# Scheduling priorities for the delta rule's chains and units, and a router that multiplies in four column tiles

## The chip, the cores and the metric

One program runs on one core of a Trainium2 chip. The metric is the device time of one execution in microseconds (us). Three runs of the kernel before took 2969.64, 2970.99 and 2975.12 us; the median is 2970.99 us.

## The reference, cut to what matters

The model has two layers on 512 latent tokens and 256 context tokens, 1024 wide. Each layer is a mixer, a residual, and an expert-choice feed-forward (16 experts, each takes the 64 latent tokens, and in layer 0 also the 32 context tokens, that score highest for it).

The router scores tokens before the experts can start:

```python
aff = jax.nn.softmax(jnp.einsum('bnd,de->bne', h, w_router), axis=-1)   # 1024 -> 16 columns
gate, idx = lax.top_k(jnp.swapaxes(aff, 1, 2), cap)
```

The mixer of layer 1 has a window attention (8 heads, blocks of 128 tokens) and a delta rule (RWKV-7: 8 heads of 64, forward and backward over the tokens):

```python
sa = einsum('bhvk,bhk->bhv', S, -kk)
S  = S * dec + sa[..., None] * (kk * a) + v[..., None] * k      # token after token
y  = einsum('bhvk,bhk->bhv', S, r)
```

Both results, side by side, are multiplied by an output matrix and added to the residual.

## The kernel before, in words

The program is: mixer 0 (to about 460 us), its output projection with the routers of layer 0 (`out_proj`, L741 on), the experts of layer 0 (`moe(0)`), mixer 1 (`mixer1`, about 1440 to 2230 us) with the routers of layer 1, and the experts of layer 1 (`moe(1)`).

A scheduler puts the instructions in order when the program is built. Every instruction has a priority, by default its place in the order in which the Python code issues it (its trace). On each engine the scheduler takes, of the instructions whose inputs are ready by its own clock, the one that was traced first. The result is one fixed order for each engine and each DMA queue: on the chip an engine waits at the head of its queue, also where a later instruction would be ready. Only TensorE in `moe` is written out by hand.

Mixer 1 is traced as rounds of a loop over Python generators (`while` at L1563). In one round every generator takes one step:

- `chain(d, u, j)` for each of four units (direction d, head group u): the serial part of the delta rule, two halves of three steps each (`an`, `RH`, `pu`, `UV`, `pn`, `N1`; L1416 to L1454) and one step for the output `ysb` (L1456 to L1474). There are 24 chains, six for each (d, u), each after the one before it.
- `prep(sl, ...)`: a unit of 128 tokens is made ready for its chain. It loads keys and rates (`AR`, `BK`, `UV`), makes the Gram matrices (`gr`), and inverts a triangular matrix by five doublings (`pf`, `Qc`, `px`, `X`, `Zbd`), and ends with `Zf` (L1412). There are 24 preps in two slots, in three once the front is done. A prep needs a free set of buffers, which the end of an earlier chain gives back.
- `front()`: projections (`pj`, L926), their features for the delta rule (`features`, L948 on), then the projections for the window attention. The features of head pair p reach a prep through DRAM.
- `win_attend` (L1176 on): 32 heads times blocks, one each round, from the round after the front's end. Its buffers lie where the front's were, and the PSUM pools are cut anew there (`open_ps(4, 2)`, L1587).
- when the window attention is done, the output weights `wo` are loaded into its place (L1599, L739); `finish(lt)` (L1478) normalizes a tile of `ysb`; `projected(t, halves)` (L1543) multiplies half a tile (window half `winT`, delta half `rwT`) by `wo`.

When all chains and `finish` are done, the slots' memory becomes the ring for the experts' weights: `x` is loaded back (L1632) and the first weight blocks (`we`, 2 MB each; L1914) follow on the same queue, SP. The ring holds six blocks, two more lie in a second pool. The routers of layer 1 run beside the last projections.

`route_tile` (L1664) norms a tile, transposes it (`htp`), scales it into `ht`, and multiplies: eight matmuls `lg` with a 128-column piece of `ht` stationary and 16 router columns moving (L1688). A float32 matmul is two passes in the trace, so a tile has 16 passes. The router columns `wr` lie in a pool that lives through the whole program, and are loaded by POOL's queue in `route_open` (L1661).

Of the kernel before, what the change touches and what calls it, by code (L numbers as in the profile page):

```python
# [11 lines left out]
F32 = mybir.dt.float32  # L12
# [87 lines left out]
class Kern:  # L100
# [690 lines left out]
    def mixer1(self):  # L791
# [325 lines left out]
        def front():  # L1117
            lats = [g for t in range(2, 6) for g in (inputs(t),)]

            def ahead():  # L1120
                if lats and next(lats[0], self) is self:
                    lats.pop(0)
            for a in (aC, aL):
                n = a[0].shape[2]
                lat = n == NLAT
                low = [fo.tile([128, n], F32, name=nm) for nm in ("tl", "al", "sgl")]
                for i, half in enumerate((1.0, None, 0.5)[:3 if lat else 2]):
                    yield from filled(shifted(12 + i, a, low[i]))
                    if half is not None:
                        nc.scalar.activation(low[i], low[i], AF.Tanh, scale=half)  # L1130
                    if i == 2:
                        nc.gpsimd.tensor_scalar(low[i], low[i], 0.5, 0.5, OP.mult, OP.add)
                for p in range(4):
                    kp, rp, vp = [fo.tile([128, n], F32, name=nm, bufs=2) for nm in ("ko", "ro", "vo")]
                    for blk, dst in ((4 + p, kp),) + (((p, rp),) if lat else ()) + ((8 + p, vp),):
                        for _ in shifted(blk, a, dst):
                            fill(FILL)
                            ahead()
                            yield
                    yield from drain()  # L1140

                    def feed(c, p=p, lat=lat, src=(kp, rp, vp), low=low):
                        s = slice(c, c + 256)
                        t0 = 2 + c // 128 if lat else 0
                        yield from features(p, t0, *[t[:, s] for t in src], [t[:, s] for t in low])
                        fed.update(((t0, p), (t0 + 1, p)))
                    work.extend(feed(c) for c in range(0, n, 256))
                if not lat:
                    yield from filled(window(aC, None))
                    while lats:  # L1150
                        ahead()
                        fill(FILL)
                        yield
                    yield from drain()

            wc = [fo.tile([128, NLAT], F32, name="wc", tag=tag, bufs=2) for tag in ("ko", "ro", "vo")]
            for i in range(2):
                nc.gpsimd.dma_start(wc[i], io["k_wc"][i])
            yield from filled(window(aL, wc))
            yield from drain()  # L1160
# [351 lines left out]
            nc.vector.tensor_tensor(ro, F[:, 1], ro, OP.mult)  # L1512

        step_ = lambda g: next(g, g) is not g
        fr = front()
        while not all((1, p) in fed for p in range(4)):
            step_(fr)
# [46 lines left out]
        while min(nj.values()) < 6 or fins or min(nfin) < 2 or win:  # L1564
            for k in units:
                if chains[k] is None and nj[k] < 6 and k + (nj[k],) in done:
                    chains[k] = chain(*k, nj[k])
                if chains[k] is not None and not step_(chains[k]):
                    chains[k] = None
                    nj[k] += 1  # L1570
                    sets.append(done[k + (nj[k] - 1,)][-1])
            for sl in slots:
                if sl.gen is None and sets:
                    ok = [k for k in units if np_[k] < min(6, nj[k] + 2)
                          and all((tile_of[k[0]][np_[k]], 2 * k[1] + i) in fed for i in range(2))]
                    if ok:
                        k = min(ok, key=lambda k: np_[k])
                        sl.gen = prep(sl, sets.pop(0), *k, np_[k])
                        np_[k] += 1
                if sl.gen is not None and not step_(sl.gen):  # L1580
                    sl.gen = None
            if fr is not None and not all([step_(fr) for _ in range(FRONT)]):
                fr = None
                fst.close()
                self.open_ps(*PS)
                mp2 = st_s.enter_context(tc.tile_pool(name="mx1b", bufs=1))
                rwT = late["rwT"] = mp2.tile([128, 4, NLAT], F32, name="rwT")  # L1587
                winT = late["winT"] = mp2.tile([128, 4, NLAT], F32, name="winT")
                self.gate_rows(1, 1, mp2)
                tc.swap_default_side()  # L1590
                slots += [open_slot(SLOTS[0] + i, st_r) for i in range(SLOTS[1])]
                sets += [open_set(SETS[0] + i, st_r) for i in range(SETS[1])]
                tc.swap_default_side()
                ww = st_w.enter_context(tc.tile_pool(name="winw", bufs=2))
                kvq = win_open(ww)
                win = [win_attend(ww, *kvq)]
            if fr is None:
                if not win and wo is None:
                    st_w.close()  # L1599
                    wo = self.out_weights(1, io["od_w_out"][0])  # L1600
                    late["fin"] = st_f.enter_context(tc.tile_pool(name="m1f", bufs=2))
                for lt in range(4):
                    if wo is not None and yset[lt] == 4 and not nfin[lt] and len(fins) < 2:
                        nfin[lt] = 1
                        fins.append((lt, finish(lt)))
            for lt, g in list(fins):
                if not step_(g):
                    fins.remove((lt, g))
                    nfin[lt] = 2
            if wo is not None and min(nj.values()) < 6:  # L1610
                if not proj:
                    ready = [t for t in (3, 4, 2, 5) if nfin[t - 2] == 2 and lack[t]] + [
                        t for t in (3, 4, 2, 5) if 4 in lack[t]]
                    if ready:
                        t = ready[0]
                        proj.append(projected(t, lack[t] if nfin[t - 2] == 2 else [4]))
                if proj and not step_(proj[0]):
                    proj.pop(0)
            win = [g for g in win if step_(g)]
# [34 lines left out]
    def route_open(self, l):  # L1654

        nc, io, tc = self.nc, self.io, self.tc
        self.rt_st = ExitStack()
        self.rtw = self.rt_st.enter_context(tc.tile_pool(name=f"rtw{l}", bufs=2))
        self.rgm, self.rsh = self.gmod(l, 1)
        self.rwr = self.small.tile([128, 8, 16], F32, name="wr", tag="wr", bufs=1)  # L1660
        nc.gpsimd.dma_start(self.rwr, io["moe_router"][l].rearrange("(k p) n -> p k n", p=128))  # L1661
        self.lgt = self.small.tile([128, 6, 16], F32, name="lgt", tag="lgt", bufs=1)

    def route_tile(self, l, t):  # L1664

        nc = self.nc
        v = 1 if t < 2 else 0
        xn = self.rtw.tile([128, D], F32, name="xn", bufs=2 if l == 0 else 3)
        self.norm_tile(self.x[t], xn)
        nc.scalar.dma_start(self.xnd[0][t] if t < 2 else self.xnd[1][t - 2], xn)  # L1670
        yield
        ht = self.rtw.tile([128, 8, 128], F32, name="ht")
        for k0 in range(0, 8, 4):
            pt = self.bank("htp")
            for i in range(4):
                nc.tensor.transpose(pt[:, 128 * i:128 * i + 128], xn[:, 128 * (k0 + i):128 * (k0 + i) + 128], self.ident)
            for i in range(4):
                k, p = k0 + i, pt[:, 128 * i:128 * i + 128]
                if k % 2:
                    nc.scalar.activation(ht[:, k], p, AF.Identity, bias=self.rsh[:, k, v:v + 1],  # L1680
                                         scale=self.rgm[:, k, v:v + 1])
                else:
                    nc.vector.tensor_scalar(ht[:, k], p, self.rgm[:, k, v:v + 1], self.rsh[:, k, v:v + 1],
                                            OP.mult, OP.add)
        yield
        lg = self.bank("lg")
        for k in range(8):
            nc.tensor.matmul(lg[:, 0:16], ht[:, k], self.rwr[:, k], start=k == 0, stop=k == 7)  # L1688
        nc.vector.tensor_copy(self.lgt[:, t], lg[:, 0:16])

    def moe(self, l, out=None):
# [460 lines left out]
```

## Time and profile before

| | us |
|---|---|
| median of three runs | 2970.99 |
| the profiled execution | 2972.21 |
| its span, first to last instruction | 2970.4 |
| PE busy / DVE busy / ACT busy / POOL busy | 2660.2 / 1322.9 / 742.6 / 471.4 |
| the granted clock of PE, mean | 0.954 |
| DMA moved | 779.47 MB, mean 262 GB/s |

The page gives busy time by engine. PE's busy time holds the latency of matmuls that overlap, so 90% busy is not 90% used. The page's slices show three kinds of stretch: the experts of layer 0 with PE at 9 tenths throughout, mixer 1 with no engine full, and the experts of layer 1 with DMA at 9 tenths and some 427 GB/s.

### The profile page before, as it was taken

What the parts mean: (1) busy time and instruction counts of PE and PEld (TensorE: products, weight loads), DVE (VectorE), ACT (ScalarE), POOL (GpSimd) and SP (SyncE); (2) the same over time, 40 slices, a digit from 0 to 9 for tenths busy, and PEclk for the clock granted to TensorE, in tenths of its full rate; (3) what the DMA queues carried; (4) which work ended last, traced back from release to release, by engine and by line L of the source; (5) the groups of instructions that cost most, each with busy time, mean ns of one, the idle gap of its engine ahead of it and who ended that gap; (6) DMA issues with size and microseconds to landing.
All of it is one profiled execution on the core that took longest, in us unless ns stands there. A gap on an engine that the chain in (4) does not pass through costs nothing.

```text
span 2970.4 us, 47837 instructions
## 1 busy us (share of the span) xinstructions
PE 2660.2 (90%) x19606; PEld 1535.4 (52%) x19606; DVE 1322.9 (45%) x3546; ACT 742.6 (25%) x1718; POOL 471.4 (16%) x591
## 2 busy tenths in 40 slices
PE   7999999799999999999878878799987987888886
PEld 4787776544444444444466656587653332333322
DVE  4323665444234334322475777677654332223312
ACT  3212444211111111101354544366321111101111
POOL 2332003200000000000283553411210000000000
PEclk9999999799999999999987988899987999999999
DMA  9765001488988988988642233310349999999997
GB/s 329 244 246 175 27 12 57 172 333 353 371 356 355 371 345 367 365 355 355 216 126 73 86 108 120 111 32 28 118 184 377 426 427 427 427 426 427 426 427 314
DMA packets 176587, 779.47 MB, mean 262 GB/s; under 512 B 24327, under 2 KB 110768, under 8 KB 133488
## 3 DMA queue, kind: packets, MB, share of 16 engines
q1 hardware_dynamic: 169200, 752.31, 64.5%
q0 software_dynamic: 3872, 12.52, 1.2%
q10 hardware_dynamic: 3296, 11.58, 1.0%
q8 instruction: 155, 2.54, 0.4%
q14 instruction: 64, 0.52, 0.1%
HBM read 745.68 MB, written 30.67 MB: 261 GB/s over the span
## 4 chain that ended last, share of the span: by engine, by line
PE 64%; DMA 19%; DVE 9%; POOL 3%; ACT 3%; issue 2%; SPq 0%; POOLq 0%; ACTq 0%; DVEq 0%
PE gu L1924 13%; PE ydn L1992 9%; DMA wd<-in_moe_w_down_dram 8%; DMA we<-in_moe_w_gate_up_dram 8%; PE guc L1937 6%; PE ydc L1996 3%; PE pj L926 3%; PE pj L411 2%; PE pj L412 2%; PE pj L413 2%; PE op L774 2%; PE op L1556 2%; PE adap L231 2%; PE sc L593 1%; PE scp L1816 1%
## 5 line engine op out<-in xcount | busy, mean ns | idle before, releaser
L1924 PE MATMUL gu<-we,xs 128*64 128x512 f32 x3072 | 687.9, 597 | 83.5 <-DMA we<-in_moe_w_gate_up_dram 83.4
L1924 PEld LDWEIGHTS gu<-we,xs 128*64 128x64 f32 x3072 | 216.7, 137 | 520.5 <-issue 408.5
L1992 PE MATMUL ydn<-wd,uT 128*64 128x512 f32 x1536 | 351.8, 600 | 14.3 <-DMA wd<-in_moe_w_down_dram 13.7
L1930 DVE TENSOR_TENSOR sg<-gu,sg 64x512 f32<-64x512 f32 x96 | 66.5, 693 | 458.4 <-ACT sg L1929 457.8
L1929 ACT ACTIVATE sg<-gu 64x512 f32<-64x512 f32 x96 | 56.8, 592 | 846.3 <-PE gu L1924 846.3
L1776 POOL DMA_INDIRECT xg<-xnd,idx x22 | 20.9, 952 | 1246.6 <-DVE gate L1781 1186.0
L1992 PEld LDWEIGHTS ydn<-wd,uT 128*64 128x64 f32 x1536 | 107.9, 137 | 205.3 <-issue 187.0
L1937 PE MATMUL guc<-we,xs 128*32 128x256 f32 x3072 | 172.6, 380 | 0.0
L926 PE MATMUL pj<-aL,wblk 128*128 128x512 f32 x504 | 158.1, 448 | 0.0
L1937 PEld LDWEIGHTS guc<-we,xs 128*32 128x32 f32 x3072 | 96.4, 110 | 68.4 <-issue 7.5
L411 PE MATMUL pj<-ah,wblk 128*128 128x384 f32 (+1 forms) x320 | 109.5, 343 | 1.4 <-ACT ah L380 1.4
L926 PEld LDWEIGHTS pj<-aL,wblk 128*128 128x128 f32 x504 | 99.0, 210 | 18.4
L412 PE MATMUL pj<-al,wblk 128*128 128x384 f32 (+1 forms) x320 | 107.9, 338 | 0.0
L413 PE MATMUL pj<-ah,wblk 128*128 128x384 f32 (+1 forms) x320 | 107.4, 336 | 0.0
L1819 DVE TENSOR_TENSOR x<-scp,x 128x512 f32<-128x512 f32 x144 | 92.3, 684 | 30.3 <-PE scp L1817 29.4
L1996 PE MATMUL ydc<-wd,uTc 128*32 128x256 f32 x1536 | 90.6, 380 | 1.4 <-DMA wd<-in_moe_w_down_dram 1.4
L1906 DVE COPY uTc<-utc 128x128 f32<-128x128 f32 x48 | 14.0, 291 | 172.6 <-PE utc L1904 172.1
L2046 DVE TENSOR_TENSOR yp<-ydn,gbc 64x512 f32<-64x512 f32 x64 | 44.1, 689 | 103.8 <-PE ydn L1992 103.3
L1796 DVE TENSOR_SCALAR xs<-xst,gm,modT 128x128 f32<-128x128 f32 (+1 forms) x88 | 34.8, 397 | 118.9 <-PE xst L1788 115.7
L1900 ACT ACTIVATE uT<-utp 128x256 f32<-128x256 f32 x96 | 36.0, 375 | 159.4 <-PE utp L1899 158.6
L1382 DVE STREAM_TRANSPOSE Zbd<-X 64x256 f16<-64x256 f16 x144 | 62.7, 436 | 24.2 <-ACT X L1376 21.8
L1996 PEld LDWEIGHTS ydc<-wd,uTc 128*32 128x32 f32 x1536 | 47.6, 110 | 43.9 <-issue 15.2
(421 smaller groups left out, 4630.4 us busy)
## 6 DMA issues: line engine op xcount, KB each, us to landing
we<-in_moe_w_gate_up_dram SPq DMA_DIRECT2D x192, 2048.0 KB, 13.5
wd<-in_moe_w_down_dram SPq DMA_DIRECT2D x95, 2048.0 KB, 11.8
adaw<-in_ada_w_dram SPq DMA_DIRECT2D x48, 1024.0 KB, 6.5
wraw<-in_od_w_in_dram SPq DMA_DIRECT2D x33, 512.0 KB, 4.2
wraw<-in_ev_w_in_dram SPq DMA_DIRECT2D x19, 512.0 KB, 6.8
fb<-B SPq DMA_DIRECT2D x24, 256.0 KB, 2.5
BK<-fb SPq DMA_DIRECT2D x24, 256.0 KB, 3.0
xnd<-xn ACTq DMA_DIRECT2D x10, 512.0 KB, 4.7
```

The lines of the kernel that those rows point to most:

```text
L231: nc.tensor.matmul(pb[32 * j:32 * j + 32], self.spad[:, k, :], w[:, 512 * j:512 * j + 512], start=k == 0, stop=k == 7, tile_position=(0, 3 ...
L411: nc.tensor.matmul(pb[:m, :384], w[:, 0, k, 0:m], ah[k][:, t], start=k == 0, stop=False)
L412: nc.tensor.matmul(pb[:m, :384], w[:, 0, k, 0:m], al[k][:, t], start=False, stop=False)
L413: nc.tensor.matmul(pb[:m, :384], w[:, 1, k, 0:m], ah[k][:, t], start=False, stop=k == 7)
L926: nc.tensor.matmul(pb[:, :n], w[:, i, k], a[j][:, k], start=k + i + j == 0, stop=k == 7 and i == 1)
L1382: nc.vector.transpose(Zd[h], X[hd[h]])
L1819: nc.vector.tensor_tensor(xs, pb, xs, OP.add)
L1924: nc.tensor.matmul(gu[64 * j:64 * j + 64, :], g.xs[:, k, 64 * a:64 * a + 64], ws[j][k], start=k == 0, stop=k == 7, tile_position=(0, 64 * j))
L1930: nc.vector.tensor_tensor(sg, gu[64:128], sg, OP.mult)
L1937: nc.tensor.matmul(guc[32 * j:32 * j + 32, 0:256], q.xs[:, k, 32 * a4:32 * a4 + 32], ws[j // 2][k][:, 256 * (j % 2):256 * (j % 2) + 256], ...
L1992: nc.tensor.matmul(y[64 * h:64 * h + 64, :], uT[:, f], wt[i][:, 512 * h:512 * h + 512], start=f == 0, stop=f == 11, tile_position=(0, 64 * h))
L1996: nc.tensor.matmul(yc[32 * j:32 * j + 32, 0:256], uTc[:, f], wt[i][:, 256 * j:256 * j + 256], start=f == 0, stop=f == 11, tile_position=(0 ...
```

## The change

Two edits. In `mixer1` the steps of chains and preps are traced at a higher priority: their instructions count as if they had been traced 4000 (chains) or 3000 (units, the preps) places earlier. The Python flow, the instructions and their data stay the same.

In the router the operands change places: the router columns, padded with zeros to 32, are stationary in one of four column tiles, and `ht` moves through (128 columns); eight such matmuls leave four partial sums of the transposed logits in one PSUM bank. ACT copies the bank out (`ls`), and one matmul with a matrix of four stacked identities (`rsum`) adds the four parts and turns them. The router columns move from the long-lived pool to the router's own, which exists only while the routers run.

```diff
+        CHAIN, UNIT = 4000, 3000
+        def first(g, ahead):
+            with tc.high_priority(offset=ahead):
+                return step_(g)
...
-                if chains[k] is not None and not step_(chains[k]):
+                if chains[k] is not None and not first(chains[k], CHAIN):
...
-                if sl.gen is not None and not step_(sl.gen):
+                if sl.gen is not None and not first(sl.gen, UNIT):
...
-        self.rwr = self.small.tile([128, 8, 16], F32, name="wr", tag="wr", bufs=1)
-        nc.gpsimd.dma_start(self.rwr, io["moe_router"][l].rearrange("(k p) n -> p k n", p=128))
+        self.rwr = self.rtw.tile([128, 8, 32], F32, name="wr", bufs=1)
+        nc.gpsimd.memset(self.rwr[:, :, 16:32], 0.0)
+        nc.gpsimd.dma_start(self.rwr[:, :, 0:16], io["moe_router"][l].rearrange("(k p) n -> p k n", p=128))
+        self.rsum = self.rtw.tile([128, 16], F32, name="rsum", bufs=1)
+        nc.vector.tensor_tensor(self.rsum, self.ident[:, 0:16], self.ident[:, 32:48], OP.add)
+        for j in (2, 3):
+            nc.vector.tensor_tensor(self.rsum, self.rsum, self.ident[:, 32 * j:32 * j + 16], OP.add)
...
+        lp = self.bank("lgp")
+        for i in range(2):
+            for j in range(4):
+                nc.tensor.matmul(lp[32 * j:32 * j + 32, 0:128], self.rwr[:, 4 * i + j], ht[:, 4 * i + j], start=i == 0,
+                                 stop=i == 1, tile_position=(0, 32 * j))
+        ls = self.rtw.tile([128, 128], F32, name="ls")
+        nc.scalar.activation(ls, lp[:, 0:128], AF.Copy)
+        yield
         lg = self.bank("lg")
-        for k in range(8):
-            nc.tensor.matmul(lg[:, 0:16], ht[:, k], self.rwr[:, k], start=k == 0, stop=k == 7)
+        nc.tensor.matmul(lg[:, 0:16], ls, self.rsum, start=True, stop=True)
         nc.vector.tensor_copy(self.lgt[:, t], lg[:, 0:16])
```

## Rows read from the trace of the kernel before

**Rows 1.** Busy time by stage: us from:to, length, PE, PEld, DVE, ACT, POOL, PEclk, DMA, GB/s.

```profile
1540.00:1912.00 372.00, 304.78 (x2462) 233.06 (x2462) 251.94 (x558) 158.63 (x386) 177.69 (x246) 0.86 0.32 94
1912.00:2097.00 185.00, 165.31 (x1849) 141.46 (x1848) 129.80 (x396) 111.40 (x334) 37.79 (x60) 0.95 0.17 51
2097.00:2203.00 106.00, 95.06 (x988) 60.40 (x988) 66.32 (x152) 29.62 (x82) 21.35 (x27) 0.89 0.33 115
2203.00:2257.50 54.50, 35.77 (x148) 24.01 (x148) 22.85 (x70) 11.58 (x26) 8.05 (x11) 0.69 0.92 358
2257.50:2970.40 712.90, 601.28 (x2813) 225.18 (x2812) 206.67 (x595) 82.83 (x165) 10.33 (x13) 0.99 0.98 414
```

**Rows 2.** SP's queue from 2060 to 2420 us: start, us, line, what was issued.

```profile
2096.69 1.02 SPq L739 DMA_DIRECT2D wo<-in_od_w_out_dram  x2
...
2201.73 1.74 SPq L1632 DMA_DIRECT2D x<-xd  x4
2203.52 1.96 SPq L1914 DMA_DIRECT2D we<-in_moe_w_gate_up_dram  x3
2230.57 0.33 SPq L255 DMA_DIRECT2D brow<-in_ada_b_dram  x1
...
2231.89 1.73 SPq L1914 DMA_DIRECT2D we<-in_moe_w_gate_up_dram  x3
```

**Rows 3.** Chain of waits, 2090 to 2262 us, in order of time: start, us, what.

```profile
2110.87 5.78 PE op L1556 x8
...
2170.80 3.52 PE op L1556 x8
...
2199.68 1.99 PE yt L1503 x32
...
2205.78 9.57 PE op L1556 x16
2215.36 1.75 PE htp L1676 x16
2217.10 3.44 PE op L1556 x8
2220.54 3.25 PE lg L1688 x30
...
2229.27 0.91 DVE op L1560
```

**Rows 4.** Stage table for line L1412 (the end of a prep): DVE busy, count.

```profile
1540.00:1912.00 372.00, 5.08 (x12) 0.86 0.32 94
1912.00:2097.00 185.00, 2.94 (x7) 0.95 0.17 51
2097.00:2203.00 106.00, 2.11 (x5) 0.89 0.33 115
```

**Rows 5.** Groups by line, 1440 to 2262 us: a doubling's steps; busy, mean ns.

```profile
L1382 DVE STREAM_TRANSPOSE Zbd<-X 64x256 f16<-64x256 f16 x144 | 62.7, 436 | 24.2 <-ACT X L1376 21.8
L1366 DVE TENSOR_TENSOR Qc<-pf,lev 128x256 f16<-128x256 f32 x120 | 47.8, 415 | 10.4 <-PE pf L1285 9.7
L1376 ACT ACTIVATE X<-px 128x256 f16<-128x256 f32 x96 | 34.8, 383 | 61.6 <-PE px L1285 50.1 <-DVE GA L1331 4.8 <-issue 2.9
```

**Rows 6.** Groups by line, 1912 to 2097 us: the window attention's matmuls; busy, mean ns.

```profile
L1200 PE MATMUL sw<-kd,qw 128*128 128x256 f32 (+1 forms) x160 | 45.3, 398 | 7.7 <-DMA qw<-wqd 6.2 <-ACT Pw L1211 1.5
L1236 PE MATMUL po<-Vw,PTw 128*128 128x64 f32 x288 | 37.8, 278 | 0.5 <-DVE GR L1331 0.4
L1224 PE MATMUL ptw<-ks,Pw 128*128 128x128 f32 x144 | 22.4, 278 | 1.4 <-ACT KBt L1350 1.2
```

**Rows 7.** PE in order of time, 1712 to 1718 us: idle before it, and until what.

```profile
1712.82 0.71 PE L926 MATMUL pj<-aL,wblk 128*128 128x512 f32 x2
1716.53 0.69 PE L1440 MATMUL pu<-RH,Zf 64*64 64x64 f32 x8 [3.00 <-DVE RH L1435]
```

**Rows 8.** Chain of waits, 480 to 570 us: the output projection and routers of layer 0.

```profile
500.51 5.46 PE op L774 x24
505.97 1.69 PE lg L1688 x16
...
546.69 1.69 PE lg L1688 x16
548.38 5.57 PE op L774 x24
...
567.26 0.09 POOL wr L1661
...
568.19 0.21 POOL we L1834
```

**Rows 9.** The page's groups: matmuls in four column tiles, their weight loads; idle before them last.

```profile
L1937 PE MATMUL guc<-we,xs 128*32 128x256 f32 x3072 | 172.6, 380 | 0.0
...
L1937 PEld LDWEIGHTS guc<-we,xs 128*32 128x32 f32 x3072 | 96.4, 110 | 68.4 <-issue 7.5
```

**Rows 10.** Tiles winT, lg and wr: an ACT copy of 128x128 out of PSUM; durations min/median/max in ns; DMA landing.

```profile
L1246 ACT ACTIVATE winT<-orw x16: 268/269/283, 1944.1 to 2097.5; 128x128 f32<-128x128 f32 x16
...
L1688 PE MATMUL lg<-wr,ht x160: 177/263/396, 505.8 to 2240.6; 128*128 128x16 f32 x160
...
DMA to landing us min/median/max: 7.4/7.8/8.2
```

## The prediction

> **What bounds the kernel now.** I read the stage table first [rows 1]. From 2257.5 us to the end DMA is 98% busy at 414 GB/s: the experts of layer 1 are bound by their weights, at a fixed distance of 712.9 us from their first matmul. So nothing is won there, and everything ahead of it that comes earlier moves the end with it. From 1540 to 2203 us no engine is full: PE's clock is granted at 0.86 to 0.95, DVE is busy for 68%, 70% and 63% of the three stages. That stretch is bound by waits.
>
> Next, what lets the experts start. In SP's queue [rows 2] the first three weight blocks leave at 2203.52, right behind the loads of x, which wait for the last `finish` (`yt` at 2199.68 in the chain, [rows 3]); the other three leave at 2231.89, behind `brow`, which waits for the eviction of the last `op` matmul at 2229.27 [rows 3]. The blocks in flight cover the 28 us from there to the first expert matmul. The mark to move is therefore the end of the last `op`, call it T: 2229.3.
>
> Then, what holds T. The window attention ends at 2097 and `wo` is issued at 2096.69 [rows 2]; its first matmul runs at 2110.87, 14.2 us later [rows 3]. From there to T pass 118.4 us. `op` itself is 4 tiles x 2 halves of the columns x 8 k x 2 passes = 128 passes at 3.52/8 = 0.44 us [rows 3], 56.3 us. The other 62 us are the delta rule: 12 of the 24 preps have ended when the front ends, 7 more end in the window stage, and 5 end after 2097 [rows 4], with their chains, `finish`, and the last two halves of `op` behind them.
>
> Why are the preps late? Two slots gave 12 preps in 372 us, three slots 7 in 185: 62 and 79 us for one. A doubling's own steps are two transposes, one `Qc`, one `X`: 2 x 0.436 + 0.415 + 0.383 = 1.7 us [rows 5], and two groups of small matmuls; five doublings with head and tail are some 25 us (an estimate from these rows). More than half of a prep's time it waits for its turn, behind work that was traced earlier. This is what a priority acts on.
>
> **The change part by part.**
>
> *Priorities, front stage (to 1912).* The `open_ps` at the front's end cuts the PSUM pools anew. A prep traced behind it needs a bank of the new pools, so it can't pass the front's end, whatever its priority. Stepping through the loop, 14 of the 24 preps are traced before it. So the stage's work stays the same, two preps more get done in it at the most, and the front, which ends the stage, has later turns while preps run and freer engines once they are out. I take 0. Bounds: 10 us early (some in-order waits of PE go), 69 us late (the third rival).
>
> *Window stage.* 10 preps are left for it or what follows, and all of them now come ahead of the window attention. An offset of 3000 places reaches across the whole stage: PE, DVE, ACT and POOL together run some 2640 instructions and passes in it [rows 1]. The preps' cost here: PE is busy 165.3 us, the window's matmuls are 45.3 + 37.8 + 22.4 = 105.5 us of it [rows 6], which leaves 59.8 us for 7 preps and chains, 8.5 us each. Three more preps than before are 26 us on PE; PE is idle for 19.7 us of the stage [rows 1], and some of the 26 us fits there. I take half, 12 us: the window attention ends at 2109. Bounds: 5 us earlier than now, 26 us later. At three slots and 35 to 40 us a prep, 10 preps take some 130 us, so the chains end near 2060, well ahead of it.
>
> *After the window attention.* `wo` still comes 14.2 us later, and this time no prep covers the wait: PE idles and starts cold. The first 16 passes took 9.57 us after an idle stretch against 2 x 3.52 [rows 3], so 2.5 us are added. Then `op` runs through: 56.3 + 2.5, three tiles of transposes at 1.75/2 [rows 3], 2.6, three routers in the new form, 2.1 (below), and 3.5 for what isn't dense: 67 us in place of 118.4. What is late next is `wo`: since the slots come free before the window's end, weight blocks may be issued ahead of it on the same queue. One is 2 MB at 414 GB/s, 5.1 us [rows 1]; I take one block, 5 us; bounds none and four (20 us).
>
> T becomes 2096.7 + 12 + 14.2 + 5 + 67 = 2194.9, against 2229.3: -34.4 us.
>
> *Routers, layer 0.* Here PE is the path: `lg` stands four times in the chain, 1.69 us each, between `op` groups [rows 8]. The new form has again 16 passes, with 32 columns stationary and 128 moving. The nearest row is `guc`: 32 stationary, 256 moving, 172.6 us/3072 = 56 ns a pass, its weight loads 96.4/3072 = 31 ns [rows 9]. Half the columns give 28 ns if columns set the pace, 31 if the weight load does, 56 if neither; I take 31, the weight load's: 0.50 us, plus two passes of the last matmul at 1.69/16 = 0.11. That makes 0.71, and saves 0.98 x 4 = 3.9 us. Bounds: 56 ns gives 0.6 x 4 = 2.4 us; if PE also waits for the copy (0.27 us, [rows 10]) with nothing in front, 1 us is left. The copy itself lies on ACT beside `op`. The last tile's `lg` runs after its `ht`, where the chain copy-matmul replaces most of it: -0.3. The load of the next layer's `wr` no longer stands on POOL ahead of the copy that lets the second weight block go (567.26 to 568.19, [rows 8]): up to -0.9, of which I take 0.3. Together -4.5 us; the experts of layer 0 pass it on.
>
> By the Trainium skill, TensorEngine Tiling (Array Packing), Key Properties, a change of the tiling mode drains TensorE, which speaks against two changes more in each tile. The rows don't show it: `guc`, in four tiles and between matmuls in two, has 0.0 us idle before 3072 passes [rows 9], though a drain could hide in busy time. If each cost `lg`'s median duration, 0.263 us [rows 10], seven tiles on the path would lose 7 x 2 x 0.263 = 3.7 us and the time would be 2936.
>
> *Routers, layer 1.* Two tiles' `lg`, 3.25 us and a little, stand on PE ahead of the last `op` [rows 3]; that is already in the 67 us. The last tile behind T: -0.4. Against it stands the new load of `wr`: it landed in 7.4 to 8.2 us [rows 10], and can be issued only when the router's pool opens, when the last `finish` has left its memory. Now that would be about 2206, due before `lg` at 2220 [rows 3]; with `finish` early it is nearer to free. I take 0; bounds 0 and 5 us, as `op` queues behind a waiting `lp`.
>
> **Sum.** -34.4 - 4.5 - 0.4 = -39.3 us on the profiled 2972.2 (span 2970.4, 1.8 around it), 1.2 above the median of the runs: 2932 against 2971.
>
> **The rivals.**
>
> 1. *The window attention takes the preps' place as the last to end.* If it pays for all five preps that now end after 2097, at 8.5 us, it ends 42 us late in place of 12; with two blocks more ahead of `wo` (10 us), the time is 2932 + 30 + 10 = 2972, no change. For it: PE is busy 89% of the window stage [rows 1]. Against: that busy time holds latency, and DVE is at 70%. Chance 0.10.
> 2. *The order hardly changes.* The scheduler takes only what is ready, and preps that lag were traced early and so are first already; then the routers' 4.9 us and their 2.3 us on PE ahead of the last `op` are all: 2964. For it: no prep passes the front's end. Against: 62 to 79 us a prep. Chance 0.08.
> 3. *The front pays (slower).* Chain steps put ahead at times that the scheduler expected, not those of the chip, hold PE with the front's projections queued behind: at 1716.53 `pu` held PE for 3.00 us, waiting for `RH` behind feature work on DVE [rows 7]. Up to 23 chain halves run in the front stage; if each waited so long, the front would end 69 us late: 3001. It decides above 39 us, 13 such waits. Against: the priority holds on DVE too, and moves `RH` ahead of that feature work. Chance 0.10.
>
> **How the numbers follow.** The forecast, 2932, has 0.72; its own range is 2900 to 2960: window -5 and `wo` not delayed give -22, the front's 10 early would reach 2900; window +26, or `wo` behind four blocks, give 2946 and 2947, both about 2960. The range for 8 in 10 reaches to the second rival and stops short of most of the first: 2896 to 2966. Within 0.2% (6 us, about what a measurement can tell) lie the first rival and half of the second: 0.14. Slower is the third, 0.10; faster the rest, 0.76.
>
> **What would show it.** Right: the last prep's `Zf` near 2050 and not behind the window attention; `wo` issued between 2090 and 2125; a stretch of idle PE until it lands; then `op` dense at 0.44 us a pass; first expert matmul near 2218; four tiled router blocks of about 0.5 us in layer 0. Wrong: a front that ends after 1925, preps that still end behind `wo`, weight blocks ahead of `wo` on SP, or PE idle ahead of chain steps.

## The result, and the profile after

The changed kernel takes 2997.7 us (median of four runs, 2991.4 to 3000.4) against 2970.3 us before on the same chip: ratio 1.0090, 95% interval 1.0065 to 1.0115. Slower by 27 us, where 39 us faster was forecast. The profiled execution, the shortest of the four, took 2991.4 us with a span of 2989.6 us, 19.2 us more than that of before; its stages can show 19 of the 27 us.

The stages were cut anew, at events that both traces have: the last store of `wqd` (the front's end), the first row maximum of the window attention, the last `winT`, the first and the last `op`. Before (length, then busy us of PE, PEld, DVE, ACT, POOL, the granted clock, DMA share, GB/s):

```profile
1540.00:1911.50 371.50, 304.28 (x2456) 232.68 (x2458) 251.82 (x558) 158.13 (x386) 177.19 (x246) 0.86 0.32 94
1911.50:1926.10 14.60, 7.17 (x30) 5.35 (x30) 5.13 (x15) 2.60 (x7) 9.46 (x11) 0.62 0.78 242
1926.10:2097.80 171.70, 158.97 (x1832) 136.79 (x1831) 125.52 (x385) 110.06 (x330) 28.83 (x49) 0.98 0.12 35
2097.80:2110.80 13.00, 11.53 (x145) 10.04 (x144) 5.51 (x15) 7.00 (x20) 1.52 (x3) 0.64 1.00 377
2110.80:2230.00 119.20, 107.42 (x926) 63.87 (x924) 70.02 (x157) 28.22 (x75) 22.77 (x28) 0.90 0.39 144
```

After, the same stages, and the experts:

```profile
1540.00:1916.60 376.60, 299.48 (x2468) 225.58 (x2468) 254.28 (x559) 158.42 (x390) 174.67 (x244) 0.88 0.30 93
1916.60:1936.60 20.00, 7.30 (x16) 5.04 (x16) 4.98 (x11) 0.00 (x0) 9.56 (x11) 0.60 0.75 236
1936.60:2119.70 183.10, 163.82 (x1820) 142.39 (x1820) 125.33 (x384) 110.32 (x329) 28.99 (x49) 0.96 0.09 27
2119.70:2134.30 14.60, 11.95 (x148) 10.68 (x144) 6.13 (x16) 6.39 (x19) 2.46 (x4) 0.64 0.67 234
2134.30:2249.00 114.70, 106.11 (x937) 61.49 (x934) 70.03 (x156) 28.89 (x77) 22.61 (x30) 0.94 0.42 158
2276.20:2989.60 713.40, 603.02 (x2813) 225.35 (x2812) 206.73 (x595) 82.79 (x165) 10.33 (x13) 0.98 0.98 414
```

The counts are the first thing to read. The window stage has 1832 passes on PE before and 1820 after, 385 and 384 instructions on DVE: no work moved from the later stages into it. The same work takes longer: 5 us more in the front, 5.4 at its end, 11.4 in the window attention, 1.6 for `wo`, and 4.5 less in `op`. The experts keep their distance (713.4 us). The ends of the preps agree: still 12, 7 and 5 in the three stages, as in [rows 4] (DVE busy, count, clock, DMA share, GB/s):

```profile
1540.00:1916.60 376.60, 5.00 (x12) 0.88 0.30 93
1916.60:2119.70 203.10, 2.97 (x7) 0.93 0.15 47
2119.70:2249.00 129.30, 2.12 (x5) 0.91 0.45 167
```

The loss at the front's end is one of queue order. SP's queue before (start, us, line, what was issued):

```profile
1903.24 0.90 SPq L261 DMA_DIRECT2D gbc<-esd  x2
1906.95 2.54 SPq L1310 DMA_DIRECT2D AR<-fa  x4
```

and after:

```profile
1914.02 2.53 SPq L1310 DMA_DIRECT2D AR<-fa  x4
...
1917.23 0.94 SPq L261 DMA_DIRECT2D gbc<-esd  x2
```

POOL's queue before (start, us, line, what was done):

```profile
1911.37 2.35 POOL L262 TENSOR_TENSOR gbc<-gbc,brow 128x1024 f32<-128x1024 f32 x1
1915.68 3.08 POOL L1168 MEMSET kd<- 64x768 f32 x4
1918.71 0.64 POOL L1176 DMA_DIRECT2D band<-in_k_m_dram  x1
```

and after:

```profile
1923.18 2.34 POOL L262 TENSOR_TENSOR gbc<-gbc,brow 128x1024 f32<-128x1024 f32 x1 [1.25 <-DMA gbc<-esd]
1925.58 0.73 POOL L1168 MEMSET kd<- 64x768 f32 x1
1926.37 1.49 POOL L1341 TENSOR_TENSOR Ttbd<-GA,m 64x256 f32<-64x256 f32 x2
1927.94 1.40 POOL L1357 TENSOR_TENSOR Zbd<-Thbd,lev 64x256 f16<-64x256 f16 x2
1929.39 0.73 POOL L1168 MEMSET kd<- 64x768 f32 x1
1930.07 0.64 POOL L1176 DMA_DIRECT2D band<-in_k_m_dram  x1
```

On SP a prep's loads now stand ahead of `gbc`; POOL waits for `gbc` to land; then a prep's `Ttbd` and `Zbd`, moved ahead by the priority, stand between the two halves of the zeroing of `kd`; `band`, which the first score tile needs, leaves at 1930.1 in place of 1918.7. Counted from the front's end that is 13.4 us in place of 7.3: the multiplication of `gbc` with its wait is 3.6 us of the difference, `Ttbd` and `Zbd` are 2.9. Further on, SP's queue after shows `wo` cut in two, its second half 10.5 us late behind a prep's load (both halves left at 2096.69 in [rows 2]):

```profile
2119.49 0.39 SPq L739 DMA_DIRECT2D wo<-in_od_w_out_dram  x1
2126.08 2.56 SPq L1310 DMA_DIRECT2D AR<-fa  x4
2128.72 1.22 SPq L1317 DMA_DIRECT2D UV<-fv  x2
2130.00 0.59 SPq L739 DMA_DIRECT2D wo<-in_od_w_out_dram  x1
...
2227.25 1.83 SPq L1936 DMA_DIRECT2D we<-in_moe_w_gate_up_dram  x3
```

In the window stage the scores wait. PE's waits there (us in total, times, longest), before:

```profile
PE pf L1285 <- DVE X L1358: 2.5, 4, 1.1
PE sw L1200 <- ACT Pw L1211: 1.5, 3, 0.6
```

and after:

```profile
PE sw L1200 <- ACT Pw L1211: 12.5, 6, 5.3
PE pf L1285 <- DVE X L1358: 4.8, 4, 1.6
```

`sw` stands at the head of PE's queue and waits for the score tile that ACT's exponential (`Pw`) has not yet read; everything behind it on PE waits too, the preps' matmuls included. This wait is 10.8 to 13.6 us in the profiles of the four kernels that have both priorities in this stage and the window's own steps traced as before (after, e2, e3, e10 below), and 1.4 to 2.3 us in before, e1, e5, e6 and e9. Other waits went, so of the 11.4 us by which the stage is longer, PE is idle for 6.6 and busy for 4.9, at a granted clock of 0.96 in place of 0.98.

The routers of layer 0 stand in the chain as tiled matmuls ([rows 8] is before):

```profile
520.74 0.77 PE lgp L1703 x16
521.50 5.66 PE op L774 x24
527.16 0.13 PE lg L1710 x2
528.21 5.49 PE op L774 x24
533.70 0.77 PE lgp L1703 x16
...
584.23 1.05 PE gu L1946
```

A tile's period on PE, from one router to the next, is 12.96 us in place of 13.57. The first expert matmul comes at 584.2 in place of 587.8.

### The profile page after: what moved, and what is told of

Same layout as the page of the kernel before. It is cut to its first block, busy times and chain, and to the rows that moved or that the text cites. A ratio compares the mean times of both kernels' runs of the same rounds, so it can differ in the third digit from the quotient of the medians.

```text
span 2989.6 us, 47897 instructions
## 1 busy us (share of the span) xinstructions
PE 2659.0 (89%) x19626; PEld 1520.1 (51%) x19626; DVE 1330.1 (44%) x3552; ACT 743.1 (25%) x1728; POOL 470.2 (16%) x593
## 4 chain that ended last, share of the span: by engine, by line
PE 65%; DMA 18%; DVE 9%; POOL 3%; ACT 2%; issue 2%; SPq 0%; POOLq 0%; ACTq 0%; DVEq 0%
PE gu L1946 14%; PE ydn L2014 9%; DMA we<-in_moe_w_gate_up_dram 8%; DMA wd<-in_moe_w_down_dram 7%; PE guc L1959 6%; PE ydc L2018 3%; PE pj L926 2%; PE pj L411 2%; PE op L774 2%; PE pj L412 2%; PE pj L413 2%; PE op L1562 2%; PE adap L231 1%; PE sc L593 1%; PE scp L1838 1%
## 5 line engine op out<-in xcount | busy, mean ns | idle before, releaser
L1285 PE MATMUL pf<-X,Thbd 128*128 128x64 f16 x480 | 38.5, 201 | 35.0 <-DVE X L1358 32.8
## 6 DMA issues: line engine op xcount, KB each, us to landing
we<-in_moe_w_gate_up_dram SPq DMA_DIRECT2D x192, 2048.0 KB, 13.4
wd<-in_moe_w_down_dram SPq DMA_DIRECT2D x95, 2048.0 KB, 11.4
```

## The experiments

All ratios are to the kernel before on the same chip, with 95% intervals. The stage lengths are from each run's trace: *front*, from the first projection of mixer 1 to the last `wqd` store; *edge*, from there to the window's first row maximum; *window*, to the last `winT`; *tail*, to the end of the last `op` (T).

| kernel | median, us | ratio | front | edge | window | tail |
|---|---|---|---|---|---|---|
| before | 2970.3 | 1 | 449.1 | 14.6 | 171.7 | 131.4 |
| after | 2997.7 | 1.0090 (1.0065 to 1.0115) | 454.0 | 20.0 | 183.1 | 128.5 |
| e1 router alone | 2964.6 | 0.9975 (0.9963 to 0.9987) | 443.1 | 14.1 | 173.8 | 127.6 |
| e2 priorities alone | 3002.5 | 1.0106 (1.0089 to 1.0123) | 457.8 | 20.2 | 184.5 | 132.1 |
| e3 after, window opened first | 2991.0 | 1.0068 (1.0051 to 1.0085) | 459.5 | 14.2 | 183.5 | 128.5 |
| e4 after, banks split | 3090.1 | 1.0398 (1.0379 to 1.0418) | 455.4 | 31.2 | 300.5 | 89.1 |
| e5 router, chains' priority | 2984.2 | 1.0048 (1.0032 to 1.0065) | 456.6 | 14.0 | 175.9 | 137.5 |
| e6 router, units' priority | 2984.7 | 1.0058 (1.0040 to 1.0075) | 450.4 | 20.2 | 175.7 | 131.4 |
| e7 after, window moved too | 3031.4 | 1.0203 (1.0188 to 1.0218) | 451.5 | 16.1 | 226.6 | 130.7 |
| e8 router, banks split | 2976.4 | 1.0015 (1.0004 to 1.0025) | 442.5 | 19.5 | 171.2 | 143.6 |
| e9 priorities in the front only | 2978.8 | 1.0025 (1.0016 to 1.0035) | 455.8 | 15.0 | 176.2 | 127.9 |
| e10 priorities after the front only | 2987.0 | 1.0049 (1.0035 to 1.0064) | 445.4 | 21.7 | 187.4 | 130.5 |
| e11 router, window opened first | 2965.6 | 0.9983 (0.9970 to 0.9995) | 446.5 | 15.6 | 171.8 | 127.7 |
| e12 as e5, 100 places | 2984.7 | 1.0041 (1.0029 to 1.0054) | 453.7 | 15.1 | 173.7 | 138.2 |

**The two edits apart.** e1 is the kernel before with the router's hunks alone, e2 with the priorities alone.

> The kernel before with the router edit alone. If the loss lies in the priorities (my theory), the router edit keeps the gain that the profile after shows in layer 0 (first expert matmul 584.2 in place of 587.8 us, 3.5 us) and 1 to 2 us behind the last `op`: about 5 us faster than before, 2965. If the router edit is the loser (a rival: three more DVE instructions ahead of the norm, the load of `wr` behind the opening of the pool), this kernel is slower than before, 2975 or more.

> The kernel before with the priorities alone. If the loss lies in the priorities, some 22 to 27 us slower than before: 2993 to 3000, with the preps' ends behind the same heads of the window attention as before and the window's first row maximum about 10 us late. If the two edits only lose together (the router's work landing on a queue that the priorities fill), within 8 us of before.

By the ratios the router gains 7.4 us and is, with e11, the fastest kernel of all. The priorities lose 31.5 us, a little more than expected. The loss is theirs alone: gain and loss add up to 1.0081, within the interval of the changed kernel.

**What ties the preps to their place.** e4 gives the window's small matmuls (`ptw`, `po`, `orw`) two banks of their own; chains and preps keep four, and of the two double tiles (`sw`, later `op`) one is left:

```diff
-                    pp = self.bank("ptw")
+                    pp = self.psw.tile([128, 512], F32, name="ptw", tag="bkw")
...
-                self.open_ps(*PS)
+                self.open_ps(4, 1)
+                self.psw = self.ps_st.enter_context(tc.tile_pool(name='psw', bufs=2, space=PSUM))
```

> The changed kernel, and in the window stage the banks of the window's small matmuls (ptw, po, orw) come from a pool of their own (two banks), the score tiles have one buffer in place of two, and chains and preps keep their four banks for themselves. If shared banks kept the preps in step with the window (theory: a bank is given out in the order of the trace, so a step that the priority moves forward still waits for the window's earlier banks), the preps now run ahead: the last ends by 2080 in place of 2199, most of them before the middle of the window attention, T is set by the window, `wo` and `op` alone, and the time is 2940 to 2975. If slots, sets or the preps' own latency pace them, they end where they did in the changed kernel (last at 2170 or later) and the time is 2990 or more.

e8 is the same split on e1, without priorities.

> The split of the banks (four for chains and preps, two for the window's small matmuls, one score tile) without any priority, with the router edit. It tells what of the 118 us lost with split and priorities is the split's: if one score tile in place of two, and one `op` tile in place of two, are the price, this kernel is as slow, 3060 or more; if moving the preps ahead of the window is the price (the window attention then runs alone and late, each head waiting for its own row maximum), this one is within 40 us of the router edit alone, 2965 to 3005, of which `op` with one tile takes some 20.

The order of DVE's queue, as the scheduler wrote it, tells how many of the window's 32 heads stand ahead of each prep's end (preps that end ahead of the first head are not listed):

```
before             4 11 13 18 24 26 32 32 32 32 32 32
after              4 10 12 17 24 26 31 32 32 32 32 32
e8 split, plain       6  9 16 22 25 30 32 32 32 32 32
e4 split, priority    1  2  3  5  6  8 10 11 13 15 16
```

So with shared banks 4000 places moved no prep by more than one head; the split alone moved them by up to five, and split and priority together moved all of them to the window's middle or ahead of it. So the shared banks, cut as they were, were the tether; slots and sets are the same in both kernels. Whether the single score tile has a share in the new order was not tried apart. The time, 3090 us, lies where the second theory put it (2990 or more), but for neither theory's reason. In e4 the preps do end earlier (the last `Zf` at 2156.7 in place of 2199.2), and all 12 in the window stage:

```profile
1915.10:2246.80 331.70, 5.02 (x12) 0.83 0.21 72
2246.80:2337.00 90.20, 0.00 (x0) 0.92 0.42 157
```

but the last `winT` comes at 2246.8, and the window stage takes 300.5 us, which reads in two parts, before and after the last `Zf`:

```profile
1946.30:2157.00 210.70, 179.42 (x2028) 145.03 (x2028) 130.87 (x374) 98.24 (x283) 40.87 (x65) 0.83 0.09 25
2157.00:2246.80 89.80, 68.76 (x524) 58.16 (x520) 39.62 (x124) 37.60 (x111) 7.64 (x8) 0.85 0.36 147
```

First the preps run with a head now and then, at a granted clock of 0.83; then the remaining half of the heads runs alone, 90 us, at 0.85. The mixed stage of before had 0.98. From the front's end to T, nearly the same work (stages as above), before:

```profile
1911.50:2229.30 317.80, 284.39 (x2923) 215.48 (x2923) 205.49 (x569) 147.87 (x429) 62.57 (x91) 0.92 0.29 99
```

and in e4:

```profile
1915.10:2336.00 420.90, 330.15 (x2909) 245.46 (x2910) 209.55 (x567) 148.09 (x424) 63.85 (x93) 0.85 0.25 90
```

Of the 103 us between them, PE is idle for 57 and busy for 46. The split is not the price: without priorities (e8) the window stage takes 171.2 us; its edge is 5 us and its tail 16 us longer than e1's, where it has one score tile and one `op` tile in place of two. Whether the single score tile makes the price of the new order higher was not tried.

**Which priority.** e5 and e6 leave one of the two offsets out; e12 is e5 with `CHAIN` at 100.

> The changed kernel with the priority on the chains alone (units as traced). Theory: the loss (33 us against the router edit alone: 5 in the front stage, 6 at its end, 11 in the window stage, 10 behind `wo`'s second half) comes from units' work put ahead of the window's loads and of its softmax on POOL, SP and DVE; the chains have few instructions and POOL's queue keeps its order, so `band` leaves within 8 us of the front's end, `sw` waits less than 5 us in the window stage, and the time is within 8 us of the router edit alone: 2960 to 2973. Rival: any step moved ahead holds an engine in order, the chains' serial steps (one waits for the other engine each time) above all; then half or more of the loss stays: 2980 or more.

> The changed kernel with the priority on the units alone (chains as traced). Theory (units' work is what displaces the window): most of the loss, 2985 to 2998, with `band` 10 us or more behind the front's end. Rival (chains' serial steps hold the engines): 2975 or less.

> As the run with the priority on the chains alone, but with 100 places in place of 4000: a reach of little more than one round of the loop. If banks and the data tether each step to its own round, so that the reach past one round does nothing, the loss is that of 4000 places: 2978 to 2988. If the far reach is what hurts, most of the loss is gone: 2970 or less.

My theory that units alone displace the window fell: against e1 the chains' priority alone costs 22 us and the units' 25 (1.0048 and 1.0058 against 0.9975). Both together cost 34, so the two losses overlap. The chains' lengthen the front (456.6 us) and the tail (137.5); the units' the front (450.4) and the edge (20.2). Why the tail of e5 and e12 is 10 us longer than e1's was not found. The window stage takes 176 us with one and 183 with both. e12 lost as much as e5: for the chains the reach does nothing beyond the first hundred places, as the banks lead one to expect.

**Where in time.** e9 and e10 switch the priority by whether the front still runs (e10 has the opposite condition):

```diff
         def first(g, ahead):
+            if fr is None:
+                return step_(g)
             with tc.high_priority(offset=ahead):
```

> Router edit, and the priorities on chains and units only while the front runs; from the front's end on they are traced as before. Theory: the front stage is stretched in every kernel with a priority (first projection to the last wqd store 450 to 460 us in seven profiles, 443 to 449 in the three without), because units' and chains' steps stand at the head of PE's queue and wait for DVE: 8 to 11 us of the loss, so 2972 to 2978, and the window stage takes the 171 to 174 us of before. Rival (the front's lateness comes with work that is done earlier, and the window stage gives it back): as the router edit alone, 2962 to 2968.

> Router edit, and the priorities only from the front's end on. Theory: the front ends as in the router edit alone (443 us behind the first projection), the step from there to the first row maximum takes 20 us in place of 14, and the window stage 182 us in place of 173, with `sw` waiting at the head of PE's queue for ACT: 15 us of loss, 2976 to 2984. Rival (all of the loss is made in the front stage, the rest only follows): 2970 or less.

They add up: 0.50% in the front, 0.74% behind it, on 0.9975; the sum, 1.0099, lies within the interval of the changed kernel. e9 has the long front and nothing else of size; its time, 2978.8, is just above what was expected. e10, a little slower than expected, has the normal front, the long edge and the longest window stage but for e4 and e7. Over all kernels the front takes 442.5 to 449.1 us without a priority in it (five profiles, median 445.4) and 450.4 to 459.5 with one (nine, median 455.4). With both priorities, what PE waits for in the front tells part of why. e1:

```profile
PE pf L1285 <- DVE X L1358: 20.7, 12, 3.1
PE bon L1040 <- DVE ro L1038: 13.5, 4, 5.7
```

e9:

```profile
PE pf L1285 <- DVE X L1358: 26.5, 10, 6.4
PE bon L1040 <- DVE ro L1038: 22.7, 6, 10.3
```

`pf`, a prep's first doubling, waits for the prep's own mask on DVE; `bon`, a matmul of the features, waits for feature work on DVE that units' and chains' steps have passed. Either stands at the head of PE's queue, with the front's projections behind it; 15 us more in the two. Some other waits are shorter: from the first projection on, PE is idle for 6.7 us more than in e1 in e9, whose front is 12.7 us longer, and for 10.8 of the 10.9 us in the changed kernel. All six kernels with both priorities in the front have these long waits (`pf` 25.6 us or more, `bon` 21.1 or more). With one priority alone they don't explain the front: in e5, e6 and e12 the two waits together are no longer than in e1, and PE is idle for less and busy for 15 to 20 us more, in e5 at a granted clock of 0.84 against 0.87; in e6 `pu` waits for `RH` for 7.6 us in place of 3.4. Why their fronts are longer is open. And in the window stage of e10:

```profile
PE sw L1200 <- ACT Pw L1211: 10.8, 6, 5.3
```

**Two repairs.** e3 opens the window attention ahead of everything; e11 does so on e1; e7 also moves the window's steps by 3000 places (the second hunk, in e7 alone).

```diff
-                kvq = win_open(ww)
+                with tc.high_priority(offset=9000):
+                    kvq = win_open(ww)
...
-            win = [g for g in win if step_(g)]
+            win = [g for g in win if first(g, UNIT)]
```

> The changed kernel, and the opening of the window attention (loads of kd, Vw, qw, band and the zeroing of kd) traced with a still higher priority, 9000 places. If the loss at the front's end is the order of SP's and POOL's queues (`band` was issued at 1930.1 in place of 1918.7, behind a wait of POOL for gbc and behind units' work), `band` leaves POOL by 1918, the window's first row maximum comes 8 to 11 us earlier than in the changed kernel, and the time falls by about as much, to 2988. If those loads are covered (the window waits for the preps that the priorities put ahead of it on PE and DVE), the time stays within 3 us of the changed kernel, 2995 or more.

> Router edit without priorities on chains and units, and only the opening of the window attention traced 9000 places ahead. Where before `band` is issued 7 us behind the front's end, it can go 2 to 4 us sooner; the kd, qw loads wait for the front's stores anyway. If the window waits for `band`, the first row maximum comes up to 4 us sooner and the time is 2960 to 2965; if it waits for the qw loads, no change to the router edit alone, 2964.

> The changed kernel, and the window attention's steps get the units' priority, 3000, and its opening 9000: all the work of the window stage is moved by about the same number of places, so its order among itself is near that of before. Theory: in the changed kernel the window's softmax steps on DVE stand behind units' steps, and `sw` at the head of PE's queue waits for the bank that ACT's `Pw` holds (12.5 us in 6 waits, 1.5 us before); this goes, the stage from the first row maximum to the last `winT` takes 172 us again in place of 183, and the time falls by 10 to 17 us to 2981 to 2988; the front stage's 5 us and the units' own lateness stay. Rival (the stage is long because preps and chains do more of their work in it): still 180 us or more, no gain.

e3 brings the edge from 20.0 back to 14.2 us (`band` leaves at 1927.1, 5.9 us behind the front's end), which shows that queue order made that part. Its time is not told apart from that of the changed kernel (the intervals overlap), and in its profile the front happened to take 5.5 us longer. In e11 the edge is no shorter than in e1, and the time is the same: without priorities nothing is to be had there. e7 went the other way than expected, to 3031: the window stage takes 226.6 us, PE's clock in it is 0.81, and `pf` waits for `X` for 20.2 us there (2.5 before). In its queue order each prep stands two heads further back than before (6 13 15 20 26 28 in place of 4 11 13 18 24 26). Moving either side against the other cost time in every kernel tried; the orders without a priority, in which the two alternate by the rounds of the loop, have the shortest window stages (171.2 to 173.8 us).

## Why the prediction was wrong

- **The step that failed is the window stage**: "10 preps are left for it or what follows, and all of them now come ahead of the window attention", chains' ends near 2060, and with them the -34.4 us. None moved by more than one of the 32 heads; the last `Zf` was at 2199.2, 20 us later than before. I had named the bank as the reason that a prep can't pass the front's end, and did not ask the same of a bank inside the stage, where the window's `ptw`, `po` and `orw` draw on the same four. e4 and e8 show that it was this, with the single score tile as the one thing not tried apart.
- **The price behind it was wrong too.** I priced preps ahead of the window at 8.5 us of PE each, 12 us in all for T, and gave a prep 35 to 40 us because "more than half of a prep's time it waits for its turn". With banks of their own and ahead of the window (e4), 12 preps took 1915 to 2157 in three slots, 60 us each, and the window attention ended 127 us later than in the changed kernel. From its first mask (`X`, L1358) to its `Zf` a prep took 48 us on the mean of these twelve, against 51 for the same twelve before: going first shortened it little, so waiting for its turn was hardly the larger part. That the rest is its own serial steps, with gaps that the window's matmuls filled, fits PE's idle time (91 us from the front's end to T in e4, 33 before), but is argued; the lower granted clock may have a part in it too.
- **The tail** was forecast at 86 us once no prep is left in it (14.2, 5 and 67). In e4 that is the case, and it took 89.1. The sum came out near, partly by luck: the first `op` came 7.5 us behind the last `winT` in place of 19.2, though six weight blocks had left ahead of `wo` (from 2175.6 on), and from it to T passed 81.6 us in place of 67, with an `op` that had one tile in place of two. In the changed kernel these terms never came into play.
- **The front stage** was taken at 0, with 69 us as the bound of the third rival. It costs 10 us between the medians of the traces and 0.50% of the time (15 us) in e9. The rival's mechanism, PE's head waiting for DVE, is the right one where both priorities act, but the waits are `pf` and `bon`, not `pu` [rows 7]; with one priority alone the cause stays open.
- **The edge** had no term. I counted weight blocks ahead of `wo` on SP (5 us) and not the preps' loads and POOL work ahead of `gbc`, `kd` and `band`: 5.4 us in the trace of after. What came ahead of `wo` was a prep's load; its 10 us were covered, the tail is not longer than in e1 by more than 1 us.
- **The second rival** had the order right: it hardly changes against the window. But it priced an order that hardly changes at nothing. Steps that move by no more than a head cost 11 us in the window stage, and the front grew by 10.
- **The routers** were forecast at -4.9 us beside what they save in the tail, and e1 measures -7.4 (3.9 to 11): the size is not told apart from the forecast, but the parts differ. `lgp` took 0.77 us where I took 0.50, a tile saves 0.61 us of PE's time and not 0.98, and the first expert matmul came 3.5 us earlier in the changed kernel (3.1 to 5.7 in the twelve profiles with the new router) in place of 4.5. At most 2.8 us of that was passed on: from it to the first projection of mixer 1 the two kernels with the old router take 874.7 and 874.4 us, the twelve with the new one 876.7 to 878.4. Why the experts of layer 0 give back some 3 us I did not find. The routers of layer 1 gained more: e1's tail is 3.8 us shorter (`lgp` 1.00 us in the chain of after, `lg` 3.25 in [rows 3]). The shorter front of e1 rests on one profile of before against it, and stays open.

By the Trainium skill, TensorEngine Tiling (Array Packing), Key Properties, a change of the tiling mode drains TensorE. The `op` groups behind a tiled router took 5.66 to 5.72 us, behind the old router 5.55 to 5.57 [rows 8]: behind a tiled router `op` took 0.17 us more at the most, where I put 0.263 for each change beside the sum. What entering the tiles costs would lie within the 0.57 to 0.97 us of `lgp` between `op` groups, and no run here tells it apart.

## What to carry to other kernels

A priority moves an instruction only as far as its buffers let it: before counting on it, ask who else draws on the same tag, and count the heads, tiles or steps between markers in the new queue order. Here two latency-bound streams that alternated filled each other's gaps: with one put ahead, the other ran alone behind it, PE idled more, its granted clock was lower, and the sum of both took longer. Where two edits come together, time each alone: here one gains 0.25% and the other loses 1.1%.

## What the runs showed of the hardware that was not expected

The granted clock differed between orders of the same work: PE was granted 0.98 in the mixed window stage of before, 0.83 and 0.85 in the two parts of e4's, and 0.81 in e7's (1820 passes in 226.6 us, PE busy for 198.2 of them), each a mean over both levels, 2.4 and 1.2 GHz:

```profile
1929.30:2155.90 226.60, 198.21 (x1820) 167.47 (x1820) 123.94 (x382) 111.42 (x326) 29.03 (x49) 0.81 0.09 28
```

Of the 43.5 us by which e7's stage is longer than that of after, PE was busy for 34.4 and idle for 9.1: the same 1820 passes, 109 ns of busy time for one in place of 90. What in the order lets the clock fall was not tried apart.
